# Row scales of a hybrid encoder block from a second, token-major copy of x, with the parameters first on the main load queue

## The chip, the cores and the metric

One core of one Trainium2 chip. The metric is the device time of one execution in microseconds (us); lower is better. Three timed runs of the kernel before gave 1272.61, 1271.04 and 1273.03 us, median 1272.61.

The core has five engines with an instruction stream each: TensorE (PE in the profile, its weight loads as PEld), VectorE (DVE), ScalarE (ACT), GpSimd (POOL) and SyncE (SP). They wait for one another on semaphores. Loads from HBM are issued by SP, ACT or POOL and carried out by DMA engines. On-chip tiles have 128 partitions; matmul results lie in PSUM.

## The reference

One layer of a streaming encoder on 256 tokens of width 2048, all float32:

```python
n = rms_norm(h, norm_mix_w)
h = h + token_mixer(n)          # n @ w_in, 8 gated-delta heads, 8 HGRN2 heads, @ w_out
n = rms_norm(h, norm_ffn_w)
h = h + squared_relu_mlp(n, w_ff1, w_ff2)
return rms_norm(h, norm_final_w)

def rms_norm(x, w):
    y = x * lax.rsqrt(jnp.mean(x * x, axis=-1, keepdims=True) + 1e-6)
    return y * w
```

What matters here is the first `rms_norm`. Its row scale, one number for each of the 256 tokens, needs the sum of the squares of 2048 features.

## The kernel before

**Layout.** The input arrives twice in HBM: `x`, token-major (256 rows of 2048), and `xt`, feature-major (16 blocks of 128 features by 256 tokens). The weights lie in tiles of 128 x 2048 (1 MB). Everything in float32 is multiplied as a rounded part and a rest (`split`, L111 to L123: ACT casts `w` to `hi` at L117, VectorE subtracts at L118 to get `lo`), so each block costs TensorE one matmul of 512 columns (hi against both parts of x, L286) and one of 256 (lo against the rounded part, L287).

**Input projection.** `project` (L270) forms one unit of 256 output columns from two weight tiles. TensorE multiplies by the unscaled x (times the norm's weight, `to_T`, L164 to L167), and the row scale is applied to the results. A first unit takes tiles 0 and 1 (`w_first`), which are loaded in quarters, interleaved with the eight pieces of `xt` that go to the tile `big` (L138 to L143), all on SP. Behind them SP loads the constants `cst` (L144), the small weights `wab` (L146), and then weight tile after weight tile (L278). The pool of weight tiles has three buffers, so that the load of the third tile waits for no other tile to be done, and the later ones wait until VectorE has finished with the tile three places before.

**Row scales.** `row_scales` (L172) is called in the first unit behind its matmuls in the code. ACT squares `big` in four pieces of 128 x 1024 (L175), VectorE adds the pieces together (L177, L179) to 256 columns, a matmul with a matrix of ones (L181) adds over the partitions and spreads the sums to all 128 of them, and two operations of ACT (L182, L183) give `rB`, the reciprocal root for each token along the columns, the same in every partition. Each unit's result is multiplied by `rB` at L295.

**Order.** The order on each engine is set by a scheduler when the program is built; it can move instructions ahead of others in the code where nothing forbids it. SP carries out its loads in the order of its stream.

**Parameters.** `prm` (L131, 83 KB: norm weights, convolution weights and the like) is loaded from ACT's stream. `to_T` needs it for every piece of x, and VectorE and ACT form some small values from it (`parameters`, L197; `ea`, L240).

**Memory.** The tile `yTa` (L94) holds the mixer's outputs for twelve heads. It is taken at the start and first written far later, in `finish_heads` (L404).

Behind the mixer's 16 heads follow the output projection (L652 to L679), the two parts of the MLP (L698 to L755) and the last norm.

Of the kernel before, what the change touches and what calls it, by code (L numbers as in the profile page):

```python
# [7 lines left out]
F32 = mybir.dt.float32  # L8
F32R = mybir.dt.float32r
AF = mybir.ActivationFunctionType  # L10
ALU = mybir.AluOpType
# [4 lines left out]
P = 128  # L16
T = 256
D = 2048
# [55 lines left out]
def hybrid_block(ctx: ExitStack, tc: tile.TileContext, x, xt, w_in, w_ab, params, w_out, w_ff1, w_ff2,  # L74
                 norm_final_w, consts, out):
    nc = tc.nc
    PE, ACT, DVE, POOL, SP = nc.tensor, nc.scalar, nc.vector, nc.gpsimd, nc.sync
# [6 lines left out]
    cpool = ctx.enter_context(tc.tile_pool(name="cpool", bufs=1))  # L84
# [6 lines left out]
    yctx = ExitStack()  # L91
    ypool = yctx.enter_context(tc.tile_pool(name="ypool", bufs=1))
    NYA = 12
    yTa = ypool.tile([P, NYA, 2 * T], F32R, tag="yT", name="yTa")  # L94
    mctx = ExitStack()
    mp = mctx.enter_context(tc.tile_pool(name="mp", bufs=1))
    psM = mctx.enter_context(tc.tile_pool(name="psM", bufs=MXB, space=PSUM))

    def wtile():
        return wpool.tile([P, 2048], F32, tag="w", name="w")  # L100
# [4 lines left out]
    def mx(name):  # L105
        return psM.tile([P, 512], F32, tag="mx", name=name)
# [19 lines left out]
    big = bpool.tile([P, 2 * D], F32, tag="h", name="big")  # L126
    x3 = big.rearrange("p (k t) -> p k t", k=KT)
    cst = cpool.tile([P, consts.shape[1]], F32, tag="cst", name="cst")
    prm = cpool.tile([P, NPARAM], F32, tag="prm", name="prm")
    w_first = [wtile() for _ in range(2)]  # L130
    ACT.dma_start(prm, params)  # L131

    def load(eng, dst, src, pieces):
        for a, b in pieces:
# [9 lines left out]
    SP.dma_start(cst, consts)  # L144
    wab = mp.tile([P, KT, 16], F32, tag="Xt", name="wab")
    SP.dma_start(wab, w_ab)  # L146

    def C(name):
        a, b = _CONST_COLS[name]
        return cst[:, a:b]  # L150

    ident, ones = C("ident"), C("ones")
    eps = C("eps")
# [4 lines left out]

    xT = bpool.tile([P, KT, 2 * T], F32R, tag="xT", name="xT")
    rB = cpool.tile([P, T], F32, tag="rB", name="rB")  # L160
    junk = mp.tile([P, 1024], F32, tag="big", name="junk")
    sums = mp.tile([P, 1024], F32, tag="u", name="sums")

    def to_T(dst, k, pt, wcol):  # L164
        ACT.activation(dst[:, k, 0:T], pt, AF.Copy, scale=wcol)
        DVE.scalar_tensor_tensor(out=dst[:, k, T:2 * T], in0=pt, scalar=wcol,
                                 in1=dst[:, k, 0:T].bitcast(F32), op0=ALU.mult, op1=ALU.subtract)  # L167
# [3 lines left out]

    def row_scales():  # L172

        for c in range(4):
            ACT.activation(junk if c else sums, big[:, c * 1024:(c + 1) * 1024], AF.Square)  # L175
            if c:
                DVE.tensor_tensor(out=sums, in0=sums, in1=junk, op=ALU.add)  # L177
        for n in (512, 256):
            DVE.tensor_tensor(out=sums[:, 0:n], in0=sums[:, 0:n], in1=sums[:, n:2 * n], op=ALU.add)  # L179
        prb = mx("prb")  # L180
        PE.matmul(prb[:, 0:T], lhsT=ones, rhs=sums[:, 0:T], start=True, stop=True)  # L181
        ACT.activation(rB, prb[:, 0:T], AF.Ln, bias=eps, scale=1.0 / D)  # L182
        ACT.activation(rB, rB, AF.Exp, scale=-0.5)  # L183

    par = cpool.tile([P, 6, NH], F32, tag="par", name="par")
    lb, oml = par[:, 0, :], par[:, 1, :]
# [10 lines left out]
    def parameters():  # L197

        DVE.tensor_copy(ones_r, ones)
        l0, l1 = cols[:, 34:42], cols[:, 42:50]  # L200
        DVE.tensor_tensor(out=par[:, 2, :], in0=l0, in1=l1, op=ALU.max)
        DVE.tensor_tensor(out=par[:, 3, :], in0=l0, in1=par[:, 2, :], op=ALU.subtract)
        DVE.tensor_tensor(out=par[:, 4, :], in0=l1, in1=par[:, 2, :], op=ALU.subtract)
        ACT.activation(par[:, 3:5, :], par[:, 3:5, :], AF.Exp)
        DVE.tensor_tensor(out=par[:, 5, :], in0=par[:, 3, :], in1=par[:, 4, :], op=ALU.add)
        DVE.reciprocal(par[:, 5, :], par[:, 5, :])
        DVE.tensor_tensor(out=lb, in0=par[:, 3, :], in1=par[:, 5, :], op=ALU.mult)
        DVE.tensor_scalar(oml, lb, -1.0, 1.0, ALU.mult, ALU.add)
        DVE.tensor_scalar(gnw[:, 0:1], cols[:, 32:33], float(P) ** -0.5, None, ALU.mult)
        DVE.tensor_copy(gnw[:, 1:2], cols[:, 33:34])  # L210
# [59 lines left out]
    def project(base, hd, chunk, dsts):  # L270
        accs = [acc_a() for _ in range(2)]
        for kh in range(2):
            first = base == 0 and hd == 0 and chunk == 0
            if first:
                w = w_first[kh]
            else:
                w = wtile()
                SP.dma_start(w, w_in[((base > 0) * NH + hd) * 4 + chunk * 2 + kh])  # L278
            for q in range(2):
                hi, lo = split(w[:, q * 1024:(q + 1) * 1024], 1024, pieces=2 if first else 1)  # L280
                hi = hi.rearrange("p (k g c) -> p k g c", k=4, g=2)
                lo = lo.rearrange("p (k g c) -> p k g c", k=4, g=2)
                for kk in range(4):
                    k = kh * 8 + q * 4 + kk
                    for g in range(2):
                        PE.matmul(accs[g], lhsT=hi[:, kk, g, :], rhs=xT[:, k, :], start=(k == 0), stop=False)  # L286
                        PE.matmul(accs[g][:, T:], lhsT=lo[:, kk, g, :], rhs=xT[:, k, 0:T],  # L287
                                  start=False, stop=(k == KT - 1))
        if first:
            row_scales()  # L290
        for g in range(2):
            lot = mp.tile([P, T], F32, tag="lot", name="lot", bufs=2)
            ACT.copy(lot, accs[g][:, T:])
            DVE.tensor_tensor(out=lot, in0=accs[g][:, 0:T], in1=lot, op=ALU.add)
            (POOL if base == 0 else DVE).tensor_tensor(out=dsts[g], in0=lot, in1=rB, op=ALU.mult)  # L295
# [15 lines left out]
    def gdn_project(hd):  # L311
        pre = mp.tile([P, 4, T], F32, tag="gx", name="pre").rearrange("p a t -> p (a t)")[:, 0:3 * (T + 3)]
        pre = pre.rearrange("p (a t) -> p a t", a=3)
        R = mp.tile([P, 4, T], F32, tag="R", name="R", bufs=RB)
        POOL.memset(pre[:, :, 0:3], 0.0)
        project(0, hd, 0, (pre[:, 0, 3:], pre[:, 1, 3:]))
        project(0, hd, 1, (pre[:, 2, 3:], R[:, 3, :]))
        return pre, R
# [59 lines left out]
            POOL.dma_start(scr_a[hd, :, b].rearrange("t s c -> s t c"),  # L378
                          view(PA(hd)[32 * b:32 * b + 32, 1, :], 32 * b, [[256, 2], [1, 32]]))

    yTb = {}

    def yT(k, a, b):
        return yTa[:, k, a:b] if k < NYA else yTb[0][:, k - NYA, a:b]

    def finish_heads(h0, nh, po, sz, scale, bank):

        n = nh * T
        if h0 >= NYA and not yTb:
            yTb[0] = ypool.tile([P, 2 * NH - NYA, 2 * T], F32R, tag="yb", name="yTb")  # L390
        sq = mp.tile([P, n], F32, tag=f"fsq{nh}", name="fsq", bufs=1)
        ACT.activation(sq, po, AF.Square)
        pm = bank("pm")[:, 0:n]
        shi = mp.tile([P, n], F32R, tag="Xn" if nh == 2 else "sh", name="shi")
        slo = mp.tile([P, n], F32R, tag="Yd" if nh == 2 else "vv", name="slo")
        ACT.copy(shi, sq)
        DVE.tensor_tensor(out=slo, in0=sq, in1=shi.bitcast(F32), op=ALU.subtract)
        PE.matmul(pm, lhsT=ones_r, rhs=shi, start=True, stop=False)
        PE.matmul(pm, lhsT=ones_r, rhs=slo, start=False, stop=True)
        ACT.activation(sq, pm, AF.Ln, bias=eps, scale=scale / P)  # L400
        ACT.activation(sq, sq, AF.Exp, scale=-0.5)
        DVE.tensor_tensor(out=sq, in0=po, in1=sq, op=ALU.mult)
        DVE.tensor_tensor(out=sq, in0=sq, in1=sz, op=ALU.mult)
        src, hs = (yTa, h0) if h0 < NYA else (yTb[0], h0 - NYA)  # L404
        yv = sq.rearrange("p (a t) -> p a t", a=nh)
        hi, lo = src[:, hs:hs + nh, 0:T], src[:, hs:hs + nh, T:]
        split(yv, None, hi, lo)
# [27 lines left out]
    def gdn_solve(Xn):  # L435
# [67 lines left out]
        for pair in range(NH // 2):  # L503
            po = sv("po")
            for n in range(2):
                hd, c = 2 * pair + n, n * T
                PE.matmul(po[:, c:c + T], lhsT=V[:, hd, 0, :], rhs=PA(hd)[:, 0, 0:T], start=True, stop=False)  # L507
                PE.matmul(po[:, c + P:c + T], lhsT=V[:, hd, 1, :], rhs=PA(hd)[:, 0, T:384], start=False, stop=True)
            finish_heads(2 * pair, 2, po, SZ[:, 2 * pair:2 * pair + 2, :].rearrange("p a t -> p (a t)"), 1.0 / P, sv)
# [109 lines left out]
        finish_heads(NH + hd, 1, po, SZ[:, (NH + hd) % NRING, :], 1.0, mx)  # L619

    st = gdn_project(0)
    parameters()
    gates()
    for n in range(2 * NH):
# [24 lines left out]
    op = octx.enter_context(tc.tile_pool(name="op", bufs=1))  # L649
    sqj = op.tile([P, 1024], F32, tag="sqj", name="sqj")  # L650
    fs = cpool.tile([P, 16], F32, tag="fs", name="fs")
    for nh in range(2):  # L652
        accs = [acc_a() for _ in range(4)]
        for kp in range(8):
            w = wtile()
            SP.dma_start(w, w_out[nh * 8 + kp])
            for kk in range(2):
                k = 2 * kp + kk
                hi, lo = split(w[:, kk * 1024:(kk + 1) * 1024], 1024)
                for hf in range(2):  # L660
                    for a, ww in ((0, hi), (T, hi), (0, lo)):
                        st = yT(k, a + hf * P, a + hf * P + P)
                        for c in range(2):
                            PE.matmul(accs[2 * hf + c], lhsT=st, rhs=ww[:, c * 512:(c + 1) * 512],  # L664
                                      start=(k == 0 and a == 0 and ww is hi), stop=(k == 2 * NH - 1 and ww is lo))
# [6 lines left out]
        for k2 in range(4):  # L672
            pt = acc_b()
            for kk in range(2):
                k = nh * 8 + k2 * 2 + kk
# [4 lines left out]
    for hf in range(2):  # L680
        DVE.tensor_tensor(out=fs[:, 4 + hf:5 + hf], in0=fs[:, 2 * hf:2 * hf + 1], in1=fs[:, 2 * hf + 1:2 * hf + 2],
                          op=ALU.add)
# [15 lines left out]
    for fg in range(NF // 4):  # L698
        accs = [acc_a() if fg % 2 == 0 else acc_b() for _ in range(4)]
        for kq in range(4):  # L700
            w = wtile()
            SP.dma_start(w, w_ff1[fg * 4 + kq])
            for q in range(2):
                hi, lo = split(w[:, q * 1024:(q + 1) * 1024], 1024)
                for kk in range(2):
                    k = 4 * kq + 2 * q + kk
# [28 lines left out]
    for f in range(NF):  # L735
# [4 lines left out]
        n = f - (NF - TAIL)  # L740
# [124 lines left out]
```

## Time and profile before

| | before |
|---|---|
| timed runs | 1271.04, 1272.61, 1273.03 us |
| the profiled execution | 1271.04 us, its span 1269.3 us |
| TensorE granted clock, mean over the span | 0.994 |
| HBM read | 225.83 MB, 180 GB/s over the span |
| first matmul | 6.03 us |
| TensorE without work at the start of the third weight tile | 0.67 us |
| weight tiles of 1 MB | 62 of w_in, 16 of w_out, 128 of w_ff, median 4.9 us from issue to landing |

The span runs from the first to the last instruction of the profiled execution; 1.7 us of its time lie around it. In rows of a timeline the numbers are the start and the length in us, then engine, line, operation, the tile written and the tiles read, sizes, how many, and in brackets the idle time of the engine ahead of it and what ended that. In a table by stage each engine has its busy time and, in brackets, its instructions, followed by the granted clock of TensorE, the mean busy share of the DMA engines, and GB/s. A chain of waits follows back from the last instruction what released each.

### The profile page before, as it was taken

The page shows a single profiled execution, that of the slowest core. Times are in us where ns is not written, and L with a number is a line of the kernel's source. Part 1 is how long each engine was busy: PE and PEld are TensorE (multiplying, and loading weights), DVE is VectorE, ACT ScalarE, POOL GpSimd, SP SyncE. Part 2 cuts the span into 40 slices and gives each one's busy share as a digit, 9 for nine tenths or more (in the row PEclk, how much of TensorE's full clock was granted, in tenths as well). Part 3 has the DMA queues.
Part 4 walks back from the last instruction along what each step waited for, and adds up shares of the span by engine and source line. Part 5 has one row for each costly group of instructions (what it writes and reads, how often), then busy time and mean ns, then how long its engine had stood idle before and what let it go on. Part 6 is the DMA issues. An engine that isn't in the chain of part 4 may idle for free.

```text
span 1269.3 us, 18524 instructions
## 1 busy us (share of the span) xinstructions
PE 1239.6 (98%) x7293; PEld 1050.3 (83%) x7293; DVE 855.0 (67%) x1211; ACT 673.9 (53%) x973; POOL 166.3 (13%) x216
## 2 busy tenths in 40 slices
PE   7999999998999999999999999999999999999997
PEld 5888888876788887888888888888888888888886
DVE  7789999889988996566555565555655545545556
ACT  7567677655667775455444444444444444444453
POOL 1233433278300130000000000000000000000000
PEclk9999999998999999999999999999999999999999
DMA  8455555533434544465555545555455555555552
GB/s 314 147 176 172 179 186 187 173 141 133 151 104 174 189 167 166 168 222 177 197 181 184 199 170 195 189 178 196 168 201 195 199 199 190 187 191 195 199 201 97
DMA packets 35798, 229.65 MB, mean 181 GB/s; under 512 B 4536, under 2 KB 5440, under 8 KB 8960
## 3 DMA queue, kind: packets, MB, share of 16 engines
q1 hardware_dynamic: 33408, 225.63, 50.4%
q0 software_dynamic: 1728, 2.11, 1.3%
q8 instruction: 57, 0.93, 0.3%
q10 hardware_dynamic: 576, 0.74, 0.2%
q14 instruction: 29, 0.24, 0.1%
HBM read 225.83 MB, written 2.63 MB: 180 GB/s over the span
## 4 chain that ended last, share of the span: by engine, by line
issue 62%; PE 30%; POOL 3%; DVE 2%; DMA 2%; ACT 0%; SPq 0%; POOLq 0%; ACTq 0%; DVEq 0%
PE acc L286 15%; PE acc L287 8%; PE acc L664 3%; POOL Xt L424 1%; POOL X L426 1%; DMA big<-in_xt_dram 1%; DMA w<-in_w_in_dram 1%; DVE E L568 1%; PE pk L368 1%; DVE E L553 0%; DVE lo L118 0%; PE pd L583 0%; PE pab L221 0%; PE po L507 0%; PE pk L369 0%
## 5 line engine op out<-in xcount | busy, mean ns | idle before, releaser
L118 DVE TENSOR_TENSOR lo<-w,hi 128x1024 fp32r<-128x1024 f32 (+1 forms) x416 | 517.3, 1244 | 363.5 <-ACT hi L117 362.4
L117 ACT CAST hi<-w 128x1024 fp32r<-128x1024 f32 (+1 forms) x416 | 433.2, 1042 | 442.0 <-PE accb L731 177.1
L286 PE MATMUL acc<-xT,hi 128*128 128x512 f32 x1024 | 363.3, 401 | 7.1 <-ACT hi L117 6.7
L287 PE MATMUL acc<-xT,lo 128*128 128x256 f32 x1024 | 283.9, 286 | 6.2 <-DVE lo L118 6.2
L286 PEld LDWEIGHTS acc<-xT,hi 128*128 128x128 f32 x1024 | 191.6, 191 | 47.3 <-ACT hi L117 7.3
L287 PEld LDWEIGHTS acc<-xT,lo 128*128 128x128 f32 x1024 | 194.9, 191 | 15.0 <-DVE lo L118 10.5
L709 PE MATMUL acc<-hT,hi 128*128 128x512 f32 x512 | 181.3, 399 | 0.0
L709 PE MATMUL accb<-hT,hi 128*128 128x512 f32 x512 | 180.8, 398 | 0.0
L731 PE MATMUL accb<-hi,gs 128*128 128x512 f32 x494 | 170.0, 389 | 0.0
L710 PE MATMUL accb<-hT,lo 128*128 128x256 f32 x512 | 143.2, 281 | 0.0
L710 PE MATMUL acc<-hT,lo 128*128 128x256 f32 x512 | 142.8, 281 | 0.0
L731 PE MATMUL acc<-hi,gs 128*128 128x512 f32 (+1 forms) x500 | 134.2, 388 | 0.0
L709 PEld LDWEIGHTS accb<-hT,hi 128*128 128x128 f32 x512 | 96.1, 188 | 23.9
L709 PEld LDWEIGHTS acc<-hT,hi 128*128 128x128 f32 x512 | 96.0, 188 | 23.4
L731 PEld LDWEIGHTS acc<-hi,gs 128*128 128x128 f32 x500 | 93.7, 188 | 19.3
L731 PEld LDWEIGHTS accb<-hi,gs 128*128 128x128 f32 x494 | 92.7, 188 | 19.3
L779 POOL TENSOR_TENSOR fin<-fin,cst 128x1 f32<-128x1 f32 x2 | 1.1, 564 | 773.9 <-issue 766.5
L710 PEld LDWEIGHTS acc<-hT,lo 128*128 128x128 f32 x512 | 96.5, 189 | 0.2
L710 PEld LDWEIGHTS accb<-hT,lo 128*128 128x128 f32 x512 | 96.6, 189 | 0.1
L731 PE MATMUL accb<-lo,gs 128*128 128x512 f32 x247 | 95.4, 389 | 0.0
L731 PE MATMUL acc<-lo,gs 128*128 128x512 f32 (+1 forms) x250 | 77.7, 388 | 0.0
L731 PEld LDWEIGHTS acc<-lo,gs 128*128 128x128 f32 x250 | 46.9, 188 | 9.7
(251 smaller groups left out, 1250.1 us busy)
## 6 DMA issues: line engine op xcount, KB each, us to landing
w<-in_w_ff_dram SPq DMA_DIRECT2D x128, 1024.0 KB, 4.9
w<-in_w_in_dram SPq DMA_DIRECT2D x62, 1024.0 KB, 4.9
w<-in_w_out_dram SPq DMA_DIRECT2D x16, 1024.0 KB, 4.9
big<-in_xt_dram SPq DMA_DIRECT2D x8, 256.0 KB, 6.2
w<-in_w_in_dram SPq DMA_DIRECT2D x8, 256.0 KB, 6.3
h<-in_x_dram SPq DMA_DIRECT2D x2, 1024.0 KB, 9.2
dt<-scr_g POOLq DMA_DIRECT2D x8, 128.0 KB, 5.6
nfw<-in_norm_final_w_dram SPq DMA_DIRECT2D x1, 1024.0 KB, 4.7
```

Of the source, the lines that this page charges most:

```text
L117: ACT.copy(hi, w)
L118: eng.tensor_tensor(out=lo, in0=w, in1=hi.bitcast(F32), op=ALU.subtract)
L286: PE.matmul(accs[g], lhsT=hi[:, kk, g, :], rhs=xT[:, k, :], start=(k == 0), stop=False)
L287: PE.matmul(accs[g][:, T:], lhsT=lo[:, kk, g, :], rhs=xT[:, k, 0:T], start=False, stop=(k == KT - 1))
L368: PE.matmul(pk0, lhsT=R[:, 1, 0:P], rhs=qk.rearrange("p a t -> p (a t)"), start=True, stop=True)
L424: POOL.tensor_tensor(out=t3, in0=X[:, j, j + 1:].unsqueeze(2).to_broadcast([np_, nr, ncol]), in1=X[:, j, 0:ncol].unsqueeze(1).to_broadcast ...
L426: POOL.tensor_tensor(out=X[:, j + 1:, 0:ncol], in0=X[:, j + 1:, 0:ncol], in1=t3, op=ALU.subtract)
L568: DVE.tensor_tensor(out=ev, in0=ev, in1=view(gx, 0, [[2 * m, nb], [T + m, 2], [1, m]]), op=ALU.mult)
L664: PE.matmul(accs[2 * hf + c], lhsT=st, rhs=ww[:, c * 512:(c + 1) * 512], start=(k == 0 and a == 0 and ww is hi), stop=(k == 2 * NH - 1 and ...
L709: PE.matmul(accs[f], lhsT=hi[:, cs], rhs=hT[:, k, :], start=(k == 0), stop=False)
L710: PE.matmul(accs[f][:, T:], lhsT=lo[:, cs], rhs=hT[:, k, 0:T], start=False, stop=(k == KT - 1))
L731: PE.matmul(dst, lhsT=gs[:, a + hf * P:a + hf * P + P], rhs=ww[:, at:at + n], start=(first and a == 0 and ww is hi), stop=(last and ww is lo))
```

## The change

The row scales no longer come from `big`. A tile `xr` takes the token-major `x` in two loads of 1 MB, half the tokens each, which stand on SP behind `wab` and ahead of the third weight tile. ACT squares each half in one instruction over 2048 columns that also gives the sum of each row (`accum_out`), and makes the reciprocal roots on two columns. VectorE multiplies the identity by these to get two diagonal matrices, and two matmuls of ones with them give `rB` in its old layout, which ACT copies out of PSUM. The load of `prm` moves from ACT's stream to the head of SP's. `xr` takes the place in memory of `yTa`, which is now taken after the first head's projection.

```diff
-    yTa = ypool.tile([P, NYA, 2 * T], F32R, tag="yT", name="yTa")
...
-    ACT.dma_start(prm, params)
+    SP.dma_start(prm, params)
...
     SP.dma_start(wab, w_ab)
+    xr = ypool.tile([P, 2, D], F32, tag="yT", name="xr")
+    for hf in range(2):
+        SP.dma_start(xr[:, hf, :], x[hf * P:(hf + 1) * P, :])
...
-    junk = mp.tile([P, 1024], F32, tag="big", name="junk")
-    sums = mp.tile([P, 1024], F32, tag="u", name="sums")
...
     def row_scales():
 
-        for c in range(4):
-            ACT.activation(junk if c else sums, big[:, c * 1024:(c + 1) * 1024], AF.Square)
-            if c:
-                DVE.tensor_tensor(out=sums, in0=sums, in1=junk, op=ALU.add)
-        for n in (512, 256):
-            DVE.tensor_tensor(out=sums[:, 0:n], in0=sums[:, 0:n], in1=sums[:, n:2 * n], op=ALU.add)
+        ss = cpool.tile([P, 2], F32, tag="ss", name="ss")
+        for hf in range(2):
+            ACT.activation(xr[:, hf, :], xr[:, hf, :], AF.Square, accum_out=ss[:, hf:hf + 1])
+        ACT.activation(ss, ss, AF.Ln, bias=eps, scale=1.0 / D)
+        ACT.activation(ss, ss, AF.Exp, scale=-0.5)
+        diag = mp.tile([P, 2, P], F32, tag="fsq1", name="diag")
         prb = mx("prb")
-        PE.matmul(prb[:, 0:T], lhsT=ones, rhs=sums[:, 0:T], start=True, stop=True)
-        ACT.activation(rB, prb[:, 0:T], AF.Ln, bias=eps, scale=1.0 / D)
-        ACT.activation(rB, rB, AF.Exp, scale=-0.5)
+        for hf in range(2):
+            DVE.tensor_scalar(diag[:, hf, :], ident, ss[:, hf:hf + 1], None, ALU.mult)
+            PE.matmul(prb[:, hf * P:(hf + 1) * P], lhsT=ones, rhs=diag[:, hf, :], start=True, stop=True)
+        ACT.copy(rB, prb[:, 0:T])
...
     st = gdn_project(0)
+    yT12[0] = ypool.tile([P, NYA, 2 * T], F32R, tag="yT", name="yTa")
```

`yT12` is the holder through which the later code reaches `yTa`. From `prm` on, the lines of the changed kernel have numbers one lower, and from the last line of the diff on one higher.

SP's stream at the end of the first operands: first before, then with the change. `w<-in_w_in_dram` of 128x512 is a quarter of tile 0 or 1; the rows of 128x2048 are whole tiles from the third on.

```order
L142 DMA big<-in_xt_dram 128x512
L143 DMA w<-in_w_in_dram 128x512
L144 DMA cst<-in_consts_dram 128x1366
L146 DMA wab<-in_w_ab_dram 128x256
L278 DMA w<-in_w_in_dram 128x2048 x60
```

```order
L141 DMA big<-in_xt_dram 128x512
L142 DMA w<-in_w_in_dram 128x512
L143 DMA cst<-in_consts_dram 128x1366
L145 DMA wab<-in_w_ab_dram 128x256
L148 DMA xr<-in_x_dram 128x2048 x2
L278 DMA w<-in_w_in_dram 128x2048 x60
```

The two loads of `xr` stand directly ahead of the third weight tile.

ACT's stream from the last pieces of the first unit to the third weight tile and the row scales, before and then with the change. The casts of 128x512 are quarters of tile 1, the first two of 128x1024 are the halves of the third tile.

```order
L165 ACTIVATE xT<-big,prm 128x256 x2
L117 CAST hi<-w 128x512
L175 ACTIVATE junk<-big 128x1024
L117 CAST hi<-w 128x1024 x2
L293 COPY lot<-acc 128x256 x2
L117 CAST hi<-w 128x1024 x2
L182 ACTIVATE rB<-prb,cst 128x256
L183 ACTIVATE rB<-rB 128x256
```

```order
L164 ACTIVATE xT<-big,prm 128x256 x2
L116 CAST hi<-w 128x512
L293 COPY lot<-acc 128x256 x2
L175 ACTIVATE xr,ss<-xr 128x2048 x2
L176 ACTIVATE ss<-ss,cst 128x2
L177 ACTIVATE ss<-ss 128x2
L116 CAST hi<-w 128x1024 x2
L183 COPY rB<-prb 128x256
```

The squares leave the stretch of the first operands, where they stood between the pieces (the last of four is shown), and all of the work on `xr` stands ahead of the first cast of the third tile.

TensorE's stream at the end of the first unit, with the change; `acc` holds the unit's results, and the rows behind `prb` are the first of the third weight tile.

```order
L286 MATMUL acc<-xT,hi 128x512
L287 MATMUL acc<-xT,lo 128x256
L182 MATMUL prb<-diag,cst 128x128 x2
L286 MATMUL acc<-xT,hi 128x512 x2
L287 MATMUL acc<-xT,lo 128x256 x2
```

Before, the one matmul of `prb` stood inside the third tile, behind the first two matmuls of its second half; now two stand ahead of its first.

More of the change, by code (lines that the diff above doesn't have):

```diff
@@ L379, in gdn_mix @@
                           view(PA(hd)[32 * b:32 * b + 32, 1, :], 32 * b, [[256, 2], [1, 32]]))
-    yTb = {}
+    yT12, yTb = {}, {}
     def yT(k, a, b):
-        return yTa[:, k, a:b] if k < NYA else yTb[0][:, k - NYA, a:b]
+        return yT12[0][:, k, a:b] if k < NYA else yTb[0][:, k - NYA, a:b]
     def finish_heads(h0, nh, po, sz, scale, bank):
@@ L403, in finish_heads @@
         DVE.tensor_tensor(out=sq, in0=sq, in1=sz, op=ALU.mult)
-        src, hs = (yTa, h0) if h0 < NYA else (yTb[0], h0 - NYA)
+        src, hs = (yT12[0], h0) if h0 < NYA else (yTb[0], h0 - NYA)
         yv = sq.rearrange("p (a t) -> p a t", a=nh)
```

## The prediction

> **What bounds the kernel now.** I read the head of the page first.
>
> ```profile
> span 1269.3 us, 18524 instructions
> PE 1239.6 (98%) x7293; PEld 1050.3 (83%) x7293; DVE 855.0 (67%) x1211; ACT 673.9 (53%) x973; POOL 166.3 (13%) x216
> ```
>
> TensorE has about 30 us without work in the whole span. A microsecond that another engine saves reaches the end only if TensorE was waiting for it, and a microsecond that TensorE newly waits at the start reaches the end nearly whole, because hardly any idle time lies behind it that could give it back. So the second view is what TensorE waits for in the first 60 us, where nearly all of the change lies (line; waited for; us in total, times, longest).
>
> ```profile
> PE acc L286 <- ACT hi L117: 6.7, 2, 6.0
> PE acc L287 <- DVE lo L118: 0.9, 3, 0.5
> ```
>
> The 6.0 us are the start of the program. The other wait, 0.7 us, is the place that matters. The third view is the timeline there, with the chain of waits, the issue of the two loads around it on SP, and (from the view of the weight tile in the same windows) how long they take to land.
>
> ```profile
> 21.49 0.28 PE L287 MATMUL acc<-xT,lo 128*128 128x256 f32 x1
> 22.45 0.73 PE L286 MATMUL acc<-xT,hi 128*128 128x512 f32 x2 [0.67 <-ACT hi L117]
> 21.35 2.00 ACT L117 CAST hi<-w 128x1024 fp32r<-128x1024 f32 x2 [1.85 <-DMA w<-in_w_in_dram]
> 13.42 7.85 DMA w<-in_w_in_dram
> 23.70 0.50 PE acc L287 x2
> 26.79 0.43 PE prb L181 x2
> 13.42 0.33 SPq L278 DMA_DIRECT2D w<-in_w_in_dram  x1
> 14.14 0.33 SPq L278 DMA_DIRECT2D w<-in_w_in_dram  x1
> DMA to landing us min/median/max: 7.8/7.8/7.8
> DMA to landing us min/median/max: 9.6/9.6/9.6
> ```
>
> Read it backwards: TensorE ends the first two weight tiles at 21.77 and starts on the third (w2 below) at 22.45; ScalarE could cast w2 only at 21.35, because its load, issued at 13.42, landed at 21.27. The next load (w3), issued at 14.14, landed at 23.7, 2.5 us later and in order of issue. Why 7.8 us? The table by stage shows the DMA engines (last two columns: their busy share, and GB/s).
>
> ```profile
> 7.00:9.00 2.00, 2.00 (x8) 1.57 (x8) 1.11 (x4) 2.00 (x4) 0.00 (x0) 1.00 1.03 343
> 15.00:17.00 2.00, 2.00 (x13) 1.67 (x12) 2.00 (x5) 2.00 (x4) 0.00 (x0) 1.00 1.05 427
> 17.00:19.00 2.00, 1.45 (x7) 0.67 (x5) 2.00 (x5) 2.00 (x5) 0.00 (x0) 1.00 1.05 424
> 19.00:21.00 2.00, 1.97 (x11) 1.59 (x12) 2.00 (x5) 0.50 (x1) 0.00 (x0) 1.00 1.02 426
> 21.00:22.00 1.00, 0.77 (x5) 0.40 (x3) 0.97 (x2) 0.65 (x1) 0.00 (x0) 1.00 1.00 369
> 25.00:26.00 1.00, 1.00 (x7) 0.91 (x6) 1.00 (x4) 0.00 (x0) 0.00 (x0) 1.00 0.14 57
> ```
>
> They are full from about 3 to 25 us. **The start is bound by bytes in one queue**, and w2 is the load that TensorE, with nothing else to do, waits for. ScalarE and VectorE are also busy there (columns four and three of busy time), but only work between w2's landing and its cast could move 22.45.
>
> **The change part by part.** *The second copy of x.* SP issues two 1 MB loads (xr) ahead of w2. They are 2 x 128 x 2048 x 4 bytes = 2.10 MB in rows of 8 KB, the shape of w2 and w3, so the rate is the one that ruled while those moved, 426 GB/s: 4.9 us. The dearer end is the 369 GB/s of 21 to 22 us, 5.7 us; the cheap end, a load that is hidden, is a rival below. Nothing hides it: the engines have no idle share, and TensorE's remaining work ends at 21.77 or earlier. w3 and w4 land 2.5 us apart behind w2, while one weight tile is 5.7 us of TensorE work (16 pairs of 0.355 us, below), so only w2 is late. **Term: +4.9.**
>
> *The parameters.*
>
> ```profile
> 0.80 0.39 SPq L142 DMA_DIRECT2D big<-in_xt_dram  x1
> 0.82 0.40 ACTq L131 DMA_DIRECT2D prm<-in_params_dram  x1
> 1.24 0.42 SPq L143 DMA_DIRECT2D w<-in_w_in_dram  x1
> 4.35 0.91 ACT L165 ACTIVATE xT<-big,prm 128x256 fp32r<-128x256 f32 x2 [2.28 <-DMA prm<-in_params_dram]
> ```
>
> One issue on SP is 0.44 us (1.24 - 0.80), so every operand load is issued that much later; the 83 KB are moved either way, and while they moved beside x they took a share of the engines. For w2 the cost is between nothing and 0.44 us: +0.2, the middle, since both ends are equally near. The parameters land no earlier, the first operand a little later, and the two small ScalarE operations now stand ahead of the first conversion; a first matmul some 0.4 us after 6.0 stays hidden in the wait for w2. **Term: +0.2.**
> The Trainium skill, page "DMA: Bandwidth & Descriptors", section "Issuing engines are not separate DMA queues", says that loads from ScalarE and from SP run on the same DMA engines and that a second issuer only saves issue time; by it the whole 0.4 us of issue would be lost, and the sum would be 0.2 larger. No row here separates the two.
>
> *The row scales.*
>
> ```profile
> 7.17 1.04 ACT L175 ACTIVATE sums<-big 128x1024 f32<-128x1024 f32 x1
> 11.83 1.23 DVE L177 TENSOR_TENSOR sums<-sums,junk 128x1024 f32<-128x1024 f32 x1 [0.20 <-ACT junk L175]
> 5.37 0.60 ACT L117 CAST hi<-w 128x512 fp32r<-128x512 f32 x1
> L671 ACT ACTIVATION_READ_ACCUMULATOR sqj<-h x4: 184/184/186, 505.8 to 552.4; 128x1 f32 x4
> 5.17 0.19 ACT L240 ACTIVATE ea<-prm 128x8 f32<-128x8 f32 x1
> ```
>
> Four squares (4.2 us of ScalarE) and three sums (3.7 us of VectorE) go from the first 22 us. This lets TensorE finish the first two tiles sooner, perhaps at 20, and it buys nothing, since it then waits for w2. What is added on ScalarE stands ahead of w2's cast: two squares of 2048 columns, each 1.04 + 1024 x (1.04 - 0.60)/512 = 1.9 us plus 0.18 for the sum, then two operations on two columns at 0.2. The first square runs while the second half of xr is still moving. The second starts when that half lands, 2.5 us before w2, and ends with its two followers after 2.1 + 0.4 = 2.5 us: just when w2 arrives. I take +0.1. The dear end is that xr and w2 land together, and both squares stand ahead of the cast: 4.6 us less nothing; with the 2.5 us spacing of the rows it is 0 to 0.3. The two small scalings on VectorE and the two 128-column matmuls run during w2's cast (1.05 us). The matmul they replace stood in the middle of w2 and took 0.43 of full TensorE time. **Terms: +0.1 and -0.4.** The copy of the sums to rB now stands behind two casts; its reader on GpSimd feeds work that TensorE needs only after two more tiles, 11 us on, so I cost it at nothing.
>
> *A longer idle time at TensorE.* It grows from 0.7 us to about 7 (20 to 27.5, with two small matmuls inside). The trace shows what a shorter one does (rows by stage: TensorE's busy time is the second number, the granted clock the third from the end).
>
> ```profile
> 286.60 0.39 PE L287 MATMUL acc<-xT,lo 128*128 128x256 f32 x1 [2.79 <-DVE lo L118]
> 284.60:288.00 3.40, 1.40 (x8) 1.27 (x9) 3.40 (x4) 2.10 (x6) 3.40 (x5) 1.00 0.17 34
> 288.00:291.40 3.40, 3.40 (x13) 2.69 (x11) 3.40 (x6) 0.83 (x1) 3.09 (x5) 0.50 0.73 280
> 298.25:301.65 3.40, 1.77 (x8) 1.57 (x7) 3.40 (x7) 0.27 (x1) 1.52 (x3) 0.50 0.49 137
> 301.65:305.07 3.42, 3.42 (x12) 2.84 (x12) 3.08 (x5) 2.64 (x3) 3.19 (x4) 0.50 0.42 175
> 10.22 0.63 PE L286 MATMUL acc<-xT,hi 128*128 128x512 f32 x1
> 10.86 0.63 PE L286 MATMUL acc<-xT,hi 128*128 128x512 f32 x1
> 12.22 0.40 PE L286 MATMUL acc<-xT,hi 128*128 128x512 f32 x1
> 12.57 0.40 PE L286 MATMUL acc<-xT,hi 128*128 128x512 f32 x1
> ```
>
> Stretches of half clock here are 3.4 or 6.8 us long: 3.4 us with 1.40 of work were followed by half clock; a stretch full of work ended it, one with 1.77 of work did not. The slow start of the program fits (matmuls of 0.63 until 11.5, 5.5 us after the first). At half clock a pair of matmuls takes 0.64 us (10.86 - 10.22), otherwise 0.355, so each slow microsecond loses 1 - 0.355/0.64 = 0.45. After 7 us of idleness the clock is surely down, and it comes back after the first full stretch: 3.4 to 6.8 us from the restart, 5.1 in the middle. The first 1.25 us are free, because there TensorE waits for VectorE's half of w2 anyway (22.45 to 23.70). That is (5.1 - 1.25) x 0.45 = 1.7, between 1.0 and 2.5. **Term: +1.7.**
> The Trainium skill, page "TensorE: Matmul & The Clock Gate", section "Part 1: The HAM clock gate", gives a warm-up of about 3.4 us whatever the work; by it the term would be (3.4 - 1.25) x 0.45 = 1.0 and the sum 0.7 smaller. The 5.5 us of this trace's own start speak for a longer one.
>
> *What moves elsewhere.* In the output projection some transposes stand a few matmuls earlier or later in TensorE's order; all operands are long there, and I cost it at nothing. GpSimd's order is unchanged.
>
> **Sum:** 4.9 + 0.2 + 0.1 - 0.4 + 1.7 = +6.5 us. The profiled execution took 1271.0 (its span of 1269.3 and 1.7 around it), so 1277.5 on its terms. It was the fastest of the three, whose median is 1272.6; for a median I forecast 1279.1.
>
> **The rivals.** *The clock does not fall* (or is back after one short stretch): the sum loses 1.7, +4.8, 1277.4. For it: the restart may fall just ahead of a boundary. Against: 41% of work already sufficed for a fall.
> *The squares become the wait:* should the second half of xr land with w2 and not 2.5 us ahead, the cast waits up to 2.5 us more: +9.0, 1281.6. Against: w2 and w3 land in order.
> *The later clock falls change.* The two near 288 and 298 us cost about (3.4 + 1.8 + 3.4) x 0.45 = 3.9 us. All later work is shifted, so they may go, or one more may come: +2.6 to +8.5, 1275.2 to 1281.
> *Not slower: the copy is hidden.* If the queue were not full when xr moves, w2 would land at 21.3 as now, and what is left is the matmul of 0.43 that goes: -0.4, 1272.2. It decides at whether 2.1 MB more fit before 21.3. With about 6.2 MB due by then, the rate would have to be a third higher, against busy shares of 1.02 to 1.05. Letting w2 pass xr would not do: the new matmuls for the row scales stand ahead of w2's in TensorE's order.
>
> **How the numbers follow.** The forecast has 70%, the unfallen clock 10%, the squares 8%, the later falls 6%, the hidden copy 6%. The bounds of the terms run from 4.7 + 0.5 - 0.5 = +4.7 on the fastest run (1275.7) to 5.7 + 0.4 + 0.3 + 2.5 - 0.4 = +8.5 on the slowest (1281.5); with the nearer parts of the rivals, 1275.0 to 1282.5. A measurement of this kernel can tell 0.2%, 2.5 us, from no change. Slower by more: 0.92; within: 0.06; faster: 0.02.
>
> **What would show it.** In the profile of the changed kernel: ScalarE's cast of w2 at about 26.4 released by the load or by the exponential; TensorE's first matmul on it at about 27.5, with matmuls of 0.63 for some microseconds and a granted clock of 0.50; DMA busy shares near 1 until 30; behind that the same work some 6 us later. I am wrong if w2 lands before 25, or if TensorE's order has other work in the gap.

## The result and the profile after

The changed kernel took 1279.45 us (median of 6 runs, 1277.50 to 1280.74) against 1272.04 us before (6 runs beside it, 1271.04 to 1273.03): ratio 1.0057, 95% interval 1.0044 to 1.0070. It is slower, by 7.4 us at the medians. The forecast was 1279.1 in a range of 1275.0 to 1282.5. A second measurement on another occasion, told below, gave 1.0041 (1.0028 to 1.0054).

The profiled execution took 1280.58 us. The head of its page and TensorE's waits in its first 60 us:

```profile
span 1278.8 us, 18525 instructions
PE 1242.5 (97%) x7295; PEld 1054.0 (82%) x7295; DVE 852.9 (67%) x1208; ACT 674.9 (53%) x974; POOL 168.1 (13%) x216
```

```profile
PE prb L182 <- DVE diag L181: 6.8, 1, 6.8
PE acc L286 <- ACT hi L116: 6.2, 1, 6.2
```

From L278 to the last line of the diff both kernels have the same line numbers, so L286 and L287 are the same matmuls in both.

Behind the first two tiles TensorE now waits once, for 6.8 us, and its idle time over the whole span went from 30 to 36 us. The timeline and the chain of waits show what it ends on, and the issue and landing of the third weight tile (w2) how late that is:

```profile
19.91 0.28 PE L287 MATMUL acc<-xT,lo 128*128 128x256 f32 x1
26.96 1.22 PE L182 MATMUL prb<-diag,cst 128*128 128x128 f32 x4 [6.77 <-DVE diag L181]
26.53 2.00 ACT L116 CAST hi<-w 128x1024 fp32r<-128x1024 f32 x2
14.53 9.46 DMA xr<-in_x_dram
26.38 0.21 ACT ss L177
28.18 0.85 PE acc L286 x2
29.03 0.66 PE acc L287 x2
15.17 0.33 SPq L278 DMA_DIRECT2D w<-in_w_in_dram  x1
DMA to landing us min/median/max: 11.3/11.3/11.3
```

TensorE ends the first two tiles at 20.2, 1.6 us sooner than before, and stands still until 26.96. The second half of xr lands at 24.0, ScalarE's squares and the two small operations end at 26.6, and w2, issued at 15.17, lands at 26.5, 5.2 us later than before. The two chains meet within 0.1 us. The stages around it (busy times, granted clock third from the end, DMA share and GB/s last):

```profile
19.00:21.00 2.00, 1.19 (x8) 0.80 (x6) 0.73 (x3) 0.73 (x2) 0.00 (x0) 1.00 1.02 430
21.00:23.00 2.00, 0.00 (x0) 0.00 (x0) 0.06 (x1) 1.43 (x1) 0.00 (x0) 1.00 1.01 426
23.00:25.00 2.00, 0.00 (x0) 0.00 (x0) 0.00 (x0) 1.56 (x3) 0.00 (x0) 1.00 1.05 442
25.50:32.30 6.80, 5.34 (x17) 4.38 (x18) 5.09 (x6) 4.82 (x10) 3.30 (x2) 0.51 0.83 329
```

The DMA engines are full while TensorE does nothing, and then the clock is at half for 6.8 us. How much of this reaches the end can be read at one group of matmuls that stands behind the same work in both kernels, the eight of `pg` in the gates: 42.96 before, 49.29 after, 6.3 us later.

```profile
42.96 1.06 PE L230 MATMUL pg<-cst,abt 32*128 32x16 f32 x8
```

```profile
49.29 1.06 PE L230 MATMUL pg<-cst,abt 32*128 32x16 f32 x8
```

Most of the rest of the difference between the two spans (9.5 us) comes 460 us on. There TensorE waits 2.9 us for the same cast in both kernels (first row before, second after):

```profile
501.29 1.65 PE L664 MATMUL acc<-hi,yTb 128*128 128x512 f32 x6 [2.93 <-ACT yTb L117]
```

```profile
507.51 2.93 PE L665 MATMUL acc<-hi,yTb 128*128 128x512 f32 x6 [2.94 <-ACT yTb L116]
```

Before, the six matmuls behind it ran at full clock; after, they took nearly twice as long, and at 514 us TensorE is 9.0 us late where it was 6.2 late ahead of them.

### The profile page after: what moved, and what is told of

Its sections match the earlier page's. It is cut to its first block, busy times and chain, and to the rows that moved or that the text cites. A ratio compares the mean times of both kernels' runs of the same rounds, so it can differ in the third digit from the quotient of the medians.

```text
span 1278.8 us, 18525 instructions
## 1 busy us (share of the span) xinstructions
PE 1242.5 (97%) x7295; PEld 1054.0 (82%) x7295; DVE 852.9 (67%) x1208; ACT 674.9 (53%) x974; POOL 168.1 (13%) x216
## 4 chain that ended last, share of the span: by engine, by line
issue 62%; PE 31%; POOL 3%; DMA 2%; DVE 2%; ACT 0%; SPq 0%; POOLq 0%; DVEq 0%
PE acc L286 16%; PE acc L287 8%; PE acc L665 3%; POOL Xt L424 1%; POOL X L426 1%; DMA w<-in_w_in_dram 1%; DMA xr<-in_x_dram 1%; PE pk L368 1%; DVE E L568 0%; PE pd L583 0%; PE pab L221 0%; DVE E L553 0%; PE po L507 0%; PE pk L369 0%; PE pa L598 0%
## 5 line engine op out<-in xcount | busy, mean ns | idle before, releaser
L286 PE MATMUL acc<-xT,hi 128*128 128x512 f32 x1024 | 363.8, 402 | 6.2 <-ACT hi L116 6.2
L287 PE MATMUL acc<-xT,lo 128*128 128x256 f32 x1024 | 283.7, 286 | 7.0 <-DVE lo L117 7.0
L286 PEld LDWEIGHTS acc<-xT,hi 128*128 128x128 f32 x1024 | 192.2, 191 | 46.0 <-ACT hi L116 6.2
L287 PEld LDWEIGHTS acc<-xT,lo 128*128 128x128 f32 x1024 | 195.7, 192 | 14.4 <-DVE lo L117 9.8
L710 PEld LDWEIGHTS acc<-hT,hi 128*128 128x128 f32 x512 | 96.1, 188 | 23.4
```

Source lines behind the costliest of these rows:

```text
L710: PE.matmul(accs[f], lhsT=hi[:, cs], rhs=hT[:, k, :], start=(k == 0), stop=False)
```

## The experiments

All times are compared with runs of the kernel before that were taken beside them. Positions below are from one profile of each; two profiles of the changed kernel differ by 0.6 us at `pg`, as the last experiment shows, so times decide where intervals are given.

**The loads without their use.** Two versions of the kernel before get the loads of x ahead of w2, into the place of `yTa`, and nothing reads them: two of 1 MB, or one (the second version has `range(1)` in place of `range(2)`).

```diff
-    yTa = ypool.tile([P, NYA, 2 * T], F32R, tag="yT", name="yTa")
...
     SP.dma_start(wab, w_ab)
+    xr = ypool.tile([P, 2, D], F32, tag="yT", name="xr")
+    for hf in range(2):
+        SP.dma_start(xr[:, hf, :], x[hf * P:(hf + 1) * P, :])
...
     st = gdn_project(0)
+    yT12[0] = ypool.tile([P, NYA, 2 * T], F32R, tag="yT", name="yTa")
```

> The kernel before, with the two 1 MB loads of the token-major x put ahead of the third weight tile as in the change, and used by nothing; the row scales are made as before. If the bytes in the queue are the cost: the third tile lands at about 26.2 us instead of 21.3, TensorE starts on it at about 27.4 instead of 22.4, a stretch of half clock follows the idle time, and the kernel is 5 to 7.5 us slower than before. If the squares ahead of the cast or the new matmuls ahead of the third tile are the cost: the third tile's first matmul comes within 1 us of where it was, and the time is within 1 us of before.

> The same with one unused load of 1 MB. If the wait is bytes over rate (1.05 MB at 426 GB/s): third tile 2.5 us later than before, first matmul on it at about 24.9, idle time about 3.1 us, +2.5 us in the wait. The clock is then near the edge: the 2.8 us of idle time at 283 us in the kernel before was followed by half clock, so +2.5 to +4.5 us in all. If the cost is a fixed one for any load put there, it is the same as with 2 MB, about +6.

Measured: with 2 MB 1281.06 us, ratio 1.0067 (1.0052 to 1.0082); with 1 MB 1275.71, ratio 1.0024 (1.0014 to 1.0033). The profile of the first, then of the second (issue and landing of w2, and the third tile's first matmul):

```profile
14.23 0.33 SPq L280 DMA_DIRECT2D w<-in_w_in_dram  x1
DMA to landing us min/median/max: 11.5/11.5/11.5
28.48 1.22 PE L288 MATMUL acc<-xT,hi 128*128 128x512 f32 x2 [4.04 <-ACT hi L116]
```

```profile
13.69 0.33 SPq L280 DMA_DIRECT2D w<-in_w_in_dram  x1
DMA to landing us min/median/max: 9.7/9.7/9.7
24.54 1.22 PE L288 MATMUL acc<-xT,hi 128*128 128x512 f32 x2
```

w2 lands at 21.3, 23.4 and 25.7 us with 0, 1 and 2 MB ahead of it: 2.2 us for each megabyte. **The bytes alone bring the delay; neither the squares nor the new matmuls are needed for it.** With 1 MB the reading is clean: w2's cast starts at 23.44, right at the landing, TensorE starts 2.1 us late, half clock follows for 3.4 us, and `pg` is 2.7 us late. With 2 MB the time is not a measure of the bytes alone: this version's order on ScalarE puts work on the first unit's scaled results ahead of w2's cast, which starts at 27.40, 1.7 us behind the landing; the half clock lasts 10.2 us, and `pg` is 7.9 us late.

**The two parts of the change apart.** One version of the kernel before with the parameters on SP, and the change with the parameters on ScalarE. The edit of the first; the second turns it round.

```diff
-    ACT.dma_start(prm, params)
+    SP.dma_start(prm, params)
```

> The kernel before with nothing but the parameters' load moved from ScalarE to the head of SP. If every operand load is late by the issue time of one more load, the third weight tile lands 0.2 to 0.44 us later than 21.3 and the time is 0 to 0.5 us above before. If, as the profile of the changed kernel suggests, the parameters land earlier on this queue (2.75 us there against 4.29), the first conversions start no later, and with the third tile unmoved the time is that of before.

> The change without the move of the parameters: row scales from the second copy, parameters on ScalarE's queue as before. If the copy is the whole loss, the third tile lands at about 26.3 us, TensorE starts on it at 27.5 to 28.2 at half clock, and the time is that of the changed kernel within 0.5 us (+7 on before). If the parameters' place has a share, the time is lower than the changed kernel's by it.

Measured: parameters alone 1274.14 us, ratio 1.0014 (1.0005 to 1.0023); copy alone 1277.64, ratio 1.0045 (1.0029 to 1.0060). The copy alone carries most of the loss; its interval overlaps with both of the changed kernel's, so the times don't resolve what the parameters add to it. For the copy alone, w2's issue and landing:

```profile
14.45 0.43 SPq L278 DMA_DIRECT2D w<-in_w_in_dram  x1
DMA to landing us min/median/max: 11.4/11.4/11.4
```

It lands at 25.8, 4.6 us later than before and 0.6 to 0.7 sooner than in the changed kernel. With the parameters alone it is issued at 13.99, takes 7.9 us and lands at 21.9, 0.6 later than before. Two pairs, the same 0.6: the parameters' place costs more than I had put down. The other profiles agree in the sign and less in the size: with the 2 MB ahead w2 lands at 25.7 and 25.8 with the parameters on ScalarE and at 26.4, 26.5 and 26.7 with them on SP; in the versions below with w2 ahead of x it lands at 18.3 and 18.7, and at 18.8 and 19.0.

The parameters alone cost more than the 0 to 0.5 us expected: 1.8 us by the ratio (0.6 to 2.9), 1.5 by the medians. In that version's profile it isn't w2's landing that costs:

```profile
13.93 0.47 PE L286 MATMUL acc<-xT,hi 128*128 128x512 f32 x1
23.10 0.73 PE L286 MATMUL acc<-xT,hi 128*128 128x512 f32 x2
24.90 0.50 PE L287 MATMUL acc<-xT,lo 128*128 128x256 f32 x2 [1.07 <-DVE lo L118]
```

TensorE goes on to w2 at 23.10 without a wait, because it ends the first two tiles only then, 1.3 us later than before: its matmuls of 512 columns took 0.63 us until 13.9 us and 0.40 behind that, where they became fast at 11.5 before. `pg` is 1.2 us late. Whether that slower start belongs to the parameters' place or only to this profile isn't shown; in the first profile of the changed kernel, with the parameters on SP too, they became fast at 11.5.

How busy the queue is, the stage of 4 to 8 us shows (first the two kernels with the parameters on ScalarE, before and the copy alone; then the two with them on SP, parameters alone and the changed kernel):

```profile
4.00:8.00 4.00, 1.98 (x6) 1.65 (x7) 3.26 (x14) 3.26 (x8) 0.00 (x0) 1.00 0.98 303
```

```profile
4.00:8.00 4.00, 2.02 (x6) 1.70 (x7) 3.16 (x14) 2.92 (x8) 0.00 (x0) 1.00 0.94 305
```

```profile
4.00:8.00 4.00, 2.13 (x7) 1.80 (x8) 2.37 (x7) 2.67 (x6) 0.00 (x0) 1.00 0.84 241
```

```profile
4.00:8.00 4.00, 1.79 (x5) 1.55 (x6) 2.23 (x7) 2.58 (x6) 0.00 (x0) 1.00 0.83 236
```

In the last two the engines are idle for a sixth of these 4 us and move 65 GB/s less: 0.26 MB, which at 426 GB/s would be the 0.6 us. But these four rows are the ends of a scatter. In this stage the other four profiles with the parameters on ScalarE show shares of 0.85 to 0.93 and 251 to 293 GB/s, the other four with them on SP 0.85 to 0.91 and 243 to 268. Only the first 4 us separate all twelve profiles: 144 to 153 GB/s with the parameters on ScalarE, 121 to 136 with them on SP. Where the 0.6 us is lost, and why, stays open. The parameters themselves do land sooner on SP, at 2.75 us instead of 4.3, but the first conversion then waits for x, and starts at 4.15 instead of 4.35:

```profile
2.75 0.21 ACT L240 ACTIVATE ea<-prm 128x8 f32<-128x8 f32 x1 [0.67 <-DMA prm<-in_params_dram]
4.15 0.91 ACT L164 ACTIVATE xT<-big,prm 128x256 fp32r<-128x256 f32 x2 [0.71 <-DMA big<-in_xt_dram]
```

**The clock.** The changed kernel with work for TensorE in the gap; the extra products go to a bank that nobody reads.

```diff
+WARM = 28
...
         if first:
+            warm = mx("warm")
+            for n in range(WARM):
+                PE.matmul(warm, lhsT=hi[:, n % 4, n % 2, :], rhs=xT[:, 12 + n % 4, :], start=(n == 0), stop=(n == WARM - 1))
             row_scales()
```

> The changed kernel with 28 extra matmuls of 128x512 on old operands into an unused PSUM bank, between the second and the third weight tile, about 6.6 us of TensorE work at full clock in about 7 us of waiting. If the half clock behind the idle time costs 1.7 to 2.5 us: no half clock before 100 us, matmuls of 0.40 us on the third tile, the two small matmuls of the row scales in under 0.7 us instead of 1.22, and the kernel 1.5 to 2.5 us faster than the changed one, about +4.7 us on before. If the half clock has no share in the loss: the same time as the changed kernel (+7.4), or slower by what the extra work runs over the gap.

Measured: 1276.63 us, ratio 1.0029 (1.0011 to 1.0048), against 1.0057 and 1.0041 for the changed kernel. It is lower, but the intervals overlap, and one of its 7 runs stands far off at 1269.83 (the others 1275.72 to 1278.37), so the gain is read from positions. Two stages of it, the two matmul groups behind the gap, and the group `pg`:

```profile
20.00:26.00 6.00, 6.00 (x30) 5.04 (x29) 0.79 (x2) 4.32 (x5) 0.00 (x0) 1.00 1.01 426
29.00:32.30 3.30, 3.17 (x19) 2.83 (x20) 3.30 (x4) 1.59 (x3) 3.13 (x2) 1.00 0.58 166
27.26 0.71 PE L183 MATMUL prb<-diag,cst 128*128 128x128 f32 x4 [0.75 <-DVE diag L182]
27.87 0.73 PE L287 MATMUL acc<-xT,hi 128*128 128x512 f32 x2
47.90 1.06 PE L231 MATMUL pg<-cst,abt 32*128 32x16 f32 x8
```

The clock stays up, the small matmuls take 0.71 us where they took 1.22, and `pg` comes at 47.90, 1.4 us sooner than in the changed kernel, although w2's cast starts 0.3 later here (26.79, since the copy of the first unit's results came between the two squares). So the half clock behind the gap is worth 1.4 us against that profile, 1.7 if the 0.3 is added. Against the second profile of the changed kernel (below), whose cast starts at 26.80 and whose half clock ended sooner, it is 0.8: `pg` is at 48.68 there.

**Another place for the copy.** This is the changed kernel with the third and fourth tile loaded, in its code, ahead of the constants, the small weights and x, which leaves the row scales for later. The scheduler put the constants between the two tiles.

```diff
-    SP.dma_start(cst, consts)
...
-    SP.dma_start(wab, w_ab)
...
-    for hf in range(2):
-        SP.dma_start(xr[:, hf, :], x[hf * P:(hf + 1) * P, :])
+
+    def late_loads():
+        SP.dma_start(cst, consts)
+        SP.dma_start(wab, w_ab)
+        for hf in range(2):
+            SP.dma_start(xr[:, hf, :], x[hf * P:(hf + 1) * P, :])
...
+            elif base == 0 and hd == 0:
+                w = w_next[kh]
...
         if first:
+            for n in range(2):
+                w_next.append(wtile())
+                SP.dma_start(w_next[n], w_in[2 + n])
+            late_loads()
             row_scales()
```

> The changed kernel with the loads in another order: the third weight tile directly behind the first unit's operands, then the constants, the fourth tile, the small weights, and the two loads of x. If the order of bytes in the queue is the whole loss: the third tile lands at about 19.5 us, TensorE starts on it at about 20.5 with no idle time over 1 us and no half clock there, the row scales come at about 30 and nobody waits for them, and the time is 1 to 2.5 us below before. If squaring x on ScalarE or the late row scales cost time by themselves, TensorE waits later in the first 45 us for the cast of a tile or the results' buffers, and the time is above before by that wait.

Measured: 1272.96 us, ratio 1.0005 (0.9995 to 1.0014). The loss is gone and no gain is seen: both the expected 1 to 2.5 us below before and the expectation of no wait over 1 us missed. At the third tile:

```profile
20.70 0.73 PE L292 MATMUL acc<-xT,hi 128*128 128x512 f32 x2 [1.41 <-ACT hi L116]
23.28 0.63 PE L292 MATMUL acc<-xT,hi 128*128 128x512 f32 x1
22.60:26.10 3.50, 3.50 (x13) 3.02 (x12) 1.80 (x2) 1.28 (x2) 0.00 (x0) 0.51 1.00 424
```

TensorE starts on it 1.75 us sooner than before, but a wait of 1.4 us and one of 0.5 are followed by 3.4 us of half clock, which costs an estimated 3.4 x 0.45 = 1.5 us (0.45 from the pairs of 0.64 and 0.355 us in the prediction).

**Versions that should beat both.** The kernel before without any copy, with the third tile directly behind the first operands, and the constants and small weights behind it:

```diff
-    SP.dma_start(cst, consts)
...
-    SP.dma_start(wab, w_ab)
+
+    def late_loads():
+        SP.dma_start(cst, consts)
+        SP.dma_start(wab, w_ab)
...
+            elif base == 0 and hd == 0:
+                w = w_next[kh]
...
         if first:
+            for n in range(2):
+                w_next.append(wtile())
+                SP.dma_start(w_next[n], w_in[2 + n])
+            late_loads()
             row_scales()
```

> The kernel before, no copy of x, with the third weight tile loaded directly behind the first operands and the constants and small weights behind it. The third tile then lands at about 19.5 us, before TensorE has ended the first two at 21.8. If TensorE's place at 22.4 is set by that load alone, it goes straight on: 0.7 to 1.2 us below before, no half clock before 100 us. If the squares and sums of the row scales on ScalarE and VectorE are what holds it there, the wait stays.

Measured: 1271.79 us, ratio 0.9990 (0.9981 to 0.9999). Its TensorE has no wait ahead of the third tile, and `pg` comes at 41.87, 1.1 us sooner than before, as expected.

The version with x behind two tiles, with 8 extra matmuls in the gap, and then the same with the parameters back on ScalarE:

```diff
+WARM = 8
...
         if first:
+            warm = mx("warm")
+            for n in range(WARM):
+                PE.matmul(warm, lhsT=hi[:, n % 4, n % 2, :], rhs=xT[:, 12 + n % 4, :], start=(n == 0), stop=(n == WARM - 1))
             for n in range(2):
```

```diff
-    SP.dma_start(prm, params)
+    ACT.dma_start(prm, params)
```

> The changed kernel with x behind the third and fourth weight tile, and 8 extra matmuls of 128x512 on old operands between the second and third tile, 1.9 us of TensorE work in the wait of 1.4 and 0.5 us that was left there. If the half clock from 22.6 to 26.1 us took back what the earlier third tile gained (TensorE was 1.7 us ahead of before at 21 us and 0.2 behind that at 41), TensorE is 1.5 to 2 us ahead of before at 41 us and stays so, and the time is 1 to 2 us below before, 8 to 9 below the changed kernel. If the extra matmuls only push the tile's own matmuls back, the time is that of before.

> The last version with x behind two tiles and the 8 extra matmuls, and the parameters back on ScalarE's queue. If the parameters on SP cost 0.6 us of the queue (third tile at 26.5 us in the changed kernel, at 25.8 with the parameters on ScalarE), the third tile lands at about 18.3 us instead of 19.1, TensorE is 2.2 to 2.6 us ahead of before at 41 us, and the time is 1.5 to 2.5 below before. If that 0.6 us was chance between single profiles, the third tile lands at about 19 and the time is that of the version before it, 0.5 below before.

Measured: 1272.10 us, ratio 0.9996 (0.9987 to 1.0004); with the parameters on ScalarE 1271.57, ratio 0.9988 (0.9979 to 0.9997). Expected were 1 to 2 and 1.5 to 2.5 us below before; by the medians they are 0.5 and 1.3 below, and the first isn't told from before. In the latter's profile:

```profile
18.76 2.00 ACT L117 CAST hi<-w 128x1024 fp32r<-128x1024 f32 x2 [1.71 <-DMA w<-in_w_in_dram]
18.84 1.52 PE L299 MATMUL warm<-xT,hi 128*128 128x512 f32 x6
21.60 0.40 PE L294 MATMUL acc<-xT,lo 128*128 128x256 f32 x2
20.00:28.00 8.00, 8.00 (x47) 6.99 (x46) 5.86 (x8) 4.79 (x7) 0.00 (x0) 1.00 1.02 423
```

The third tile lands at 18.7 (11.5 + 7.2), 0.3 us sooner than with the parameters on SP (19.0) and later than the 18.3 expected, and TensorE works through at full clock: its first lo matmuls of the third tile start at 21.60 against 23.70 before. The time shows 1.3 of these 2.1 us, with an interval of 0.4 to 2.7 (`pg` is no measure here, since more of the projection's matmuls stand ahead of it in this version). It is the best version that uses the copy, 0.1% below the kernel before and 0.5 to 0.7% below the changed one by their own comparisons. But the version without the copy is as good within the intervals of some 1 us, so **the second copy of x is not seen to buy anything that the order of the loads alone doesn't give.**

**The changed kernel again.**

> The changed kernel as it is, again, for the share of the loss that lies behind the first 45 us. If the start alone is the loss, every profile shows TensorE about 6.3 us (5 to 7.5 with the clock's phase) behind the kernel before at 45 us, and the median is 6 to 7 us above before; stretches of half clock near 290 to 335 and 505 us come and go from run to run in both kernels. If the change also makes those stretches longer by itself, the median is 8 or more above before, and a stretch at about 506 us is there again with its full 6.8 us.

Measured: 1278.85 us (5 runs, 1276.24 to 1279.04), ratio 1.0041 (1.0028 to 1.0054). `pg` at 48.68 is 5.7 us late, 0.6 less than in the first profile: the half clock ended at 30.5 and not 32.3. Around 508 us:

```profile
508.30:511.70 3.40, 3.40 (x12) 2.54 (x10) 1.77 (x3) 0.91 (x1) 0.00 (x0) 0.50 0.52 219
511.70:515.00 3.30, 3.30 (x17) 2.71 (x16) 1.93 (x3) 2.34 (x5) 0.00 (x0) 0.99 0.00 0
```

The stretch of half clock is there, half as long. By the two ratios the changed kernel stands 5.2 and 7.3 us above before (0.0041 and 0.0057 of 1272), by the medians 6.0 and 7.4; the start shows 5.7 and 6.3. A lengthening of the later stretches by the change itself isn't needed for it, nor excluded for a part of 1 us. The stretch near 508 us doesn't belong to the change: over 494 to 520 us the mean granted clock is 1.00 before and with the copy alone, and 0.87 to 0.93 in the other ten profiles, among them those of the parameters alone (0.87) and of the version below before that has no copy (0.93).

## Why the prediction was right

Its mechanism held: w2 waits in the queue behind 2 MB, nothing covers the wait, and TensorE restarts at half clock. That the medians (1279.45 and 1278.85) came within 0.4 us of the forecast is partly luck: by the ratios the change costs 7.3 and 5.2 us, where 6.5 was forecast. Point by point:

- *The copy, +4.9.* Measured 4.4 to 4.6 us without the parameters' share (25.7 and 25.8 against 21.3). The price was a little high: from landing to landing 2.2 us for 1.05 MB is 477 GB/s, where 426 was read from the stages. The engines weren't faster: with 2 MB unused, the stages from 21 to 26 us show 401 to 434 GB/s. Why the landing moves by less than the bytes over that rate wasn't tried.
- *The parameters, +0.2, at most 0.44.* Too small: 0.6 at w2's landing in two pairs of kernels, and above the bound, though by no more than profiles of one kernel differ (26.5 and 26.7). The bound took the issue of one more load for the only price; what else there is stays open. "The parameters land no earlier" was wrong too (2.75 against 4.3), and it hardly helped, since x then came last.
- *The squares ahead of the cast, +0.1.* Right: 24.0 for the second half, 26.6 for the last small operation, 26.5 for w2; in the second profile 24.3, 26.9 and 26.7. The estimate of 1.9 + 0.18 for a square was measured as 1.91 and 0.19.
- *The matmul that goes, -0.4, and the clock, +1.7.* Together they gave +1.0 (6.3 less 5.2 and 0.1), where the forecast had +1.3. In the second profile, where half clock lasts 3.3 us behind the restart (27.24 to 30.5) and not 5.3, they gave 0.2 (5.7 less 5.4 and 0.1), below the lower bound of 1.0 - 0.4. A full clock takes 1.4 to 1.7 us off the first profile and 0.8 off the second. What I hadn't seen is where the half clock strikes first: at the two small matmuls, which were to hide behind w2's cast. They took 1.22 us, until 28.18, while the cast's first half was done by 27.6.
- *The sum.* +6.5 was forecast for the start and 6.3 and 5.7 measured at `pg`; the copy was priced 0.3 to 0.5 too high and the parameters 0.4 too low. That these errors cancel is luck.
- *The rivals.* The hidden copy fell with w2's landing at 26.5 and the two versions of unused loads. The unfallen clock was made, not met: it took extra work to keep it up. The squares as the wait did not occur: the second half of xr landed 2.5 us ahead of w2. Their chain did release TensorE (`diag`, 26.96), but only 0.1 us behind w2's. The later clock falls did change between profiles, as the two rows at 501 and 507 us show; that they make the spread of some 3 us between the runs is likely but not shown.

The Trainium skill's page "DMA: Bandwidth & Descriptors", section "Issuing engines are not separate DMA queues", speaks of issue time alone as what another issuing engine saves. The 0.6 us measured here is above the 0.44 of one issue, but with two profiles of the changed kernel 0.2 us apart no run here shows that more than issue time is lost. On its page "TensorE: Matmul & The Clock Gate", section "Part 1: The HAM clock gate", the warm-up is some 3.4 us; here half clock lasted 3.4, 6.8 and 10.2 us in different profiles, and 5.3 us of the 6.8 in the changed kernel lay behind the restart (26.96 to 32.3), in its second profile 3.3 (27.24 to 30.5).

## What to carry to other kernels

At a start that is bound by bytes, as here, the bytes ahead of the next operand that the bounding engine needs cost their time (2.2 us for each load of 1 MB); a load that is used later belongs behind that operand, however cheap the arithmetic becomes through it. Price an idle gap of TensorE twice, once for its length and once for the half clock behind it, and look at what runs first behind the gap. Moving a small load to the head of the queue that feeds the start wasn't free here, though it was 83 KB.

## What the hardware showed beyond that

A gap of 1.4 us and one of 0.5 close by were followed by a fall to half clock (22.6 to 26.1 us in the version with x behind two tiles), while in the kernel before a gap of 2.93 us at 501 us had none and the same gap in the changed kernel had one of 6.8 us: the length of a gap doesn't decide it alone. And the profile of the kernel before that carried the prediction was at the fast end (1271.04, where the medians of 22, 27 and 14 runs beside the experiments were 1272.80, 1272.60 and 1272.88), so a sum made against it needed the shift to the median to come out right.
